# A four-group arm for expert tiles of up to 32 tokens, own index places, and a code prefetch hint

## The chip, the cores and the metric

The kernel runs on one core of a Trainium2 chip. Its time is the device time of one execution in microseconds. The engines are named as in the profile: PE (TensorE's matmuls; PEld its weight loads), DVE (VectorE), ACT (ScalarE), POOL (GpSimd) and SP (SyncE). A name with a q behind it (PEldq, SPq) is that engine's own sequencer, which works through loads of registers, branches and semaphores.

## The reference, cut to what matters

One decoder layer: a mixer (a state-space branch and an attention branch), then a mixture of experts. Only the second part is touched. 512 tokens of 1024 numbers are routed to two of sixteen experts each, with a hidden width of 512:

```python
for e in range(N_EXPERTS):
    hid = jax.nn.silu(t @ w_gate[e]) * (t @ w_up[e])
    out = out + gates[:, e:e + 1] * (hid @ w_down[e])
```

The kernel does this for the tokens that are routed to an expert alone.

## The kernel before, in words

The expert stage starts about 578 us into the span and ends near 900 us. Each expert's tokens are cut into tiles of H = 64. For each expert `body(e, 0)` always runs; `body(e, 1)` runs behind a branch on more than 64 tokens (L1354), `body(e, 2)` behind a second one, nested in it, on more than 128 (L1356). What is above 192 tokens goes through a loop that this input doesn't enter (L1421 is its branch). The counts lie in `cnti`; each engine loads the one that its branch needs into a register (L1347).

A body does this, in the order of the code:

- `tile_ranks` makes one-hot matrices on DVE (L1151) that say which token lands in which slot of a tile.
- `tile_tokens` turns them into indices and gate weights: five small matmuls on PE (L1156, L1158), a conversion (L1160) and a reduce (L1165) on DVE, and then a gather on POOL (an indirect DMA, L1161) that brings the 64 tokens of the tile, two half rows each, into `xgs`. Body 0 of expert e does it for tiles 0 and 1 of expert e + 2, body 1 for tile 2 of its own expert, whether or not that holds tokens.
- `up` multiplies the 64 tokens by gate and up (L1288). The tokens are the stationary operand, 64 columns wide; gate's product goes to the lower 64 partitions of a bank and up's to the upper 64.
- `hidden` applies silu on ACT (L1292) and multiplies on DVE (L1293). Two small copies follow (L1328, L1329), which keep the tile's indices and gate weights.
- `down` (L1303) is that of the tile before this one, and `add` scales its result (L1307) and adds it to the output by an indirect DMA on POOL (L1308).
- `x_columns` transposes gathered tokens on PE (L1181) for ACT to copy (L1182): in body 0 the first two tiles of the next expert, in body 1 tile 2 of this one. It waits for their gathers.
- `hidden_columns` transposes the hidden product (L1297) and copies it on DVE (L1298) for the next `down`.

Within a body, `in_order` keeps PE, DVE and ACT to the order of the code, save what the scheduler may place elsewhere for other engines. Between one branch and the next it can also set a body's first matmuls ahead: the first few matmuls of the next expert's `up` stand ahead of the branch L1354 on PE. The weights of the experts are loaded by SP in pieces of 1 MB, far ahead of their use, and `ew.drop` frees their places. Indices live in three sets of places used in turn (`ixs[e % 3]`), so writing one waits for the scatter that used the place before.

Of the kernel before, what the change touches and what calls it, by code (L numbers as in the profile page):

```python
# [17 lines left out]
P = 128  # L18
# [10 lines left out]
UNIT = 512  # L29
EVAC = 400  # L30
DUE = 8, 4, 4
H = P // 2
INL = 3
MAXO = 10

# [72 lines left out]
def hybrid_layer(ctx: ExitStack, tc: tile.TileContext, A, out):  # L108
# [128 lines left out]
    class Stream:  # L237
# [7 lines left out]
        def add(self, units, loads, parts):  # L245
            for n, part in enumerate(parts):
                self.parts.append((len(self.raws), n == len(parts) - 1) + part)
            self.raws.append((units, loads))
# [96 lines left out]
    class Experts:  # L345
# [18 lines left out]
        def up(self, e, k):  # L364

            assert self.nload >= 6 * e + 4
            return [self.piece(6 * e + 2 * (k // 4) + n)[:, k % 4 * FF:(k % 4 + 1) * FF] for n in range(2)]
# [750 lines left out]
    def clear_early(BM):  # L1118

        for et in kinds:  # L1120
            xgs[et] = BM.alloc(1).ap
        sgs.extend(BM.alloc(1).ap for _ in range(2))
        for a in (*xgs.values(), *sgs):
            nc.gpsimd.memset(a, 0.0)

# [14 lines left out]
        ew.raws.append(xrc[1].ap)  # L1140
        ew.load()

    ixs = [[rtile(f"ix{e}{t}", [P, 1], I32) for t in range(INL)] for e in range(3)]
    gws = [[rtile(f"gw{e}{t}", [P, 1]) for t in range(INL)] for e in range(3)]
    ixl = [rtile(f"ixl{e}", [P, 1], I32) for e in range(2)]
    gwl = [rtile(f"gwl{e}", [P, 1]) for e in range(2)]
    rkx = rtile("rkx", [P, NT])

    def onehots(oh, ranks, slots):
# [17 lines left out]
    def oh_of(e, t):  # L1167
        return ohs[t if e or t == 2 else 3 + t]
# [2 lines left out]
        onehots(oh_of(e, t), rk[:, :, e], itbs[t])  # L1171

    def tile_tokens(e, t, n0=0, n1=5):
        tokens(oh_of(e, t), lambda c: aux[:, c, e, :], ixs[e % 3][t], gws[e % 3][t], xgs[e % 2, t], n0, n1,
               128 + 8 * (e % 2 * 3 + t))

    def x_columns(xg, xT):
# [26 lines left out]

    NB = S // H - INL
    cnt = rtile("cnt", [P, 16])
    cnti = rtile("cnti", [P, 17], I32)
    ext = rtile("ext", [P, NB, 16])
    nov = rtile("nov", [P, 1])

# [6 lines left out]
    def over_counts():  # L1217
        nc.vector.tensor_copy(cnt, pc[:, 0:16])
        nc.vector.tensor_copy(cnti[:, 0:16], cnt)
        for b in range(NB):  # L1220
            nc.vector.tensor_scalar(ext[:, b, :], cnt, float((b + INL) * H) + 0.5, None, op0=ALU.is_gt)
        nc.vector.tensor_reduce(nov, ext, axis=AX.XY, op=ALU.add)
        nc.vector.tensor_copy(cnti[:, 16:17], nov)

    jk = FM.alloc(2)
    t3.append(FM.alloc(2))
# [58 lines left out]
    def up(strm, e, xT, bank):  # L1285
        for k in range(KT):
            for n, w in enumerate(strm.up(e, k)):
                nc.tensor.matmul(bank[n * H:(n + 1) * H], xT[:, (2 * (k % 4) + k // 4) * H:(2 * (k % 4) + k // 4 + 1) * H],  # L1288
                                 w, start=(k == 0), stop=(k == KT - 1))

    def hidden(bank, sg):
        nc.scalar.activation(sg[H:P], bank[0:H], AF.Silu)  # L1292
        nc.vector.tensor_tensor(sg[H:P], sg[H:P], bank[H:P], op=ALU.mult)  # L1293
# [6 lines left out]
    def down(strm, e, bank):  # L1300
        for k in range(4):
            for n, w in enumerate(strm.down(e, k)):
                nc.tensor.matmul(bank[n * H:(n + 1) * H], hidT[0][:, k, :], w, start=(k == 0), stop=(k == 3))  # L1303

    def add(bank, yo, ix, gw):

# [5 lines left out]
    def body(e, t):  # L1312

        bank, by, yo, sg = bgu[t], bys[t % 2], yos[t % 2], sgs[t % 2]
        with in_order((ET.PE, ET.DVE, ET.Activation)):
            if t == 0:
                if e + 2 < NE:
                    for u in range(2):
                        tile_ranks(e + 2, u)
                tile_ranks(e, 2)  # L1320
            if t == 1:
                tile_tokens(e, 2)
            up(ew, e, xTs[e % 2, t], bank)
            if e == 0 and t == 0:
                for e_, t_ in early:
                    tile_tokens(e_, t_, 2, 5)
            hidden(bank, sg)
            nc.vector.tensor_copy(ixl[e % 2], ixs[e % 3][t])  # L1328
            nc.vector.tensor_copy(gwl[e % 2], gws[e % 3][t])  # L1329
            if t:  # L1330
                down(ew, e, by)
                add(by, yo, ixs[e % 3][t - 1], gws[e % 3][t - 1])
            elif e:
                down(ew, e - 1, by)
                add(by, yo, ixl[1 - e % 2], gwl[1 - e % 2])
                ew.drop(2)
            if t == 0 and e + 1 < NE:
                for u in range(2):
                    x_columns(xgs[1 - e % 2, u], xTs[1 - e % 2, u])
            if t == 1:  # L1340
                x_columns(xgs[e % 2, 2], xTs[e % 2, 2])
            hidden_columns(sg)
            if t == 0 and e + 2 < NE:
                for u in range(2):
                    tile_tokens(e + 2, u)

    n_toks = [nc.values_load(cnti[0:1, e:e + 1], min_val=0, max_val=S) for e in range(NE)]  # L1347
    n_over = nc.values_load(cnti[0:1, 16:17], min_val=0, max_val=MAXO)
    n_raw = len(ew.raws)
    assert n_raw >= 18  # L1350

    for e in range(NE):
        body(e, 0)
        with tc.If(n_toks[e] > H):  # L1354
            body(e, 1)
            with tc.If(n_toks[e] > 2 * H):  # L1356
                body(e, 2)
        if e + 1 < NE:
            ew.drop(4)
    down(ew, NE - 1, bys[0])  # L1360
    add(bys[0], yos[0], ixl[(NE - 1) % 2], gwl[(NE - 1) % 2])


    spare = [ew.piece(6 * (NE - 3) + n) for n in range(18)]
# [103 lines left out]
```

## Time and profile before

| | us |
|---|---|
| median of 3 runs | 934.03 |
| lowest and highest | 932.49, 934.2 |
| the profiled execution | 932.47 |
| its span, first to last instruction | 930.6 |
| PE busy in the span | 842.8 (91%) |
| DVE busy | 540.6 (58%) |
| ACT busy | 309.6 (33%) |
| POOL busy | 101.3 (11%) |

Of the 16 DMA engines' time, queue q1 (loads that SP issues) takes 55.3% and q0 (gathers and scatters) 7.6%. The profile is one execution; a group's row gives the busy time of its instructions, the mean of one, and the idle time of the engine just ahead of them with what ended it. Matmuls are pipelined, so that records overlap: the time that a run of them takes is read from starts in the timeline, not from the sum of durations.

### The profile page before, as it was taken

The page shows a single profiled execution, that of the slowest core. Times are in us where ns is not written, and L with a number is a line of the kernel's source. Part 1 is how long each engine was busy: PE and PEld are TensorE (multiplying, and loading weights), DVE is VectorE, ACT ScalarE, POOL GpSimd, SP SyncE. Part 2 cuts the span into 40 slices and gives each one's busy share as a digit, 9 for nine tenths or more (in the row PEclk, how much of TensorE's full clock was granted, in tenths as well). Part 3 has the DMA queues.
Part 4 walks back from the last instruction along what each step waited for, and adds up shares of the span by engine and source line. Part 5 has one row for each costly group of instructions (what it writes and reads, how often), then busy time and mean ns, then how long its engine had stood idle before and what let it go on. Part 6 is the DMA issues. An engine that isn't in the chain of part 4 may idle for free. (4 is left out here: it accounts for less than half of the span.)

```text
span 930.6 us, 11855 instructions
## 1 busy us (share of the span) xinstructions
PE 842.8 (91%) x4216; PEld 542.3 (58%) x4216; DVE 540.6 (58%) x1310; ACT 309.6 (33%) x558; POOL 101.3 (11%) x113
## 2 busy tenths in 40 slices
PE   2899989999999999999999995999999999999850
PEld 1678768887666677878888883433343333333320
DVE  6849879858876687977745784423333223122216
ACT  5438788444643432432233451101110010001100
POOL 1001000000000000000000011122222221122210
PEclk9899999999999999999999985999999999999985
DMA  9951457213122248795445289598799998459734
GB/s 288 340 147 52 152 173 191 87 40 103 46 69 72 91 140 268 222 302 160 147 143 186 106 305 398 211 385 296 247 391 386 385 381 287 145 192 314 278 71 180
DMA packets 137170, 194.88 MB, mean 209 GB/s; under 512 B 11819, under 2 KB 85723, under 8 KB 137073
## 3 DMA queue, kind: packets, MB, share of 16 engines
q1 hardware_dynamic: 127040, 174.81, 55.3%
q0 software_dynamic: 9584, 18.45, 7.6%
q8 instruction: 46, 0.75, 0.3%
q10 hardware_dynamic: 464, 0.58, 0.2%
q14 instruction: 36, 0.29, 0.1%
HBM read 189.04 MB, written 13.16 MB: 217 GB/s over the span
## 5 line engine op out<-in xcount | busy, mean ns | idle before, releaser
L398 PE MATMUL bank<-rm,rm 128*128 128x512 f32 x512 | 206.2, 407 | 0.4 <-ACT rm L431 0.4
L400 PE MATMUL bank<-rm,rm 128*128 128x512 f32 x512 | 205.8, 402 | 0.0
L399 PE MATMUL bank<-rm,rm 128*128 128x512 f32 x512 | 204.8, 400 | 0.2 <-DVE rm L433 0.2
L1288 PE MATMUL bank<-fm,fm 128*64 128x512 f32 x408 | 123.8, 601 | 4.4 <-issue 2.0
L1288 PE MATMUL bank<-bm,fm 128*64 128x512 f32 x360 | 118.4, 597 | 1.6 <-PEq L1356 0.4
L234 DVE TENSOR_TENSOR rm<-fm,rm 128x1024 fp32r<-128x1024 f32 (+1 forms) x76 | 87.6, 1163 | 42.9 <-ACT rm L233 27.3
L398 PEld LDWEIGHTS bank<-rm,rm 128*128 128x128 f32 x512 | 97.8, 192 | 21.9 <-issue 3.1
L399 PEld LDWEIGHTS bank<-rm,rm 128*128 128x128 f32 x512 | 97.4, 190 | 21.5 <-issue 2.1
L400 PEld LDWEIGHTS bank<-rm,rm 128*128 128x128 f32 x512 | 97.1, 190 | 20.8 <-issue 2.3
L1293 DVE TENSOR_TENSOR bm<-bm,bank 64x512 f32<-64x512 f32 x24 | 16.6, 692 | 152.4 <-ACT bm L1292 143.4
L233 ACT CAST rm<-fm 128x1024 fp32r<-128x1024 f32 (+1 forms) x76 | 75.2, 1007 | 79.5 <-PE bank L399 59.5
L1292 ACT ACTIVATE bm<-bank 64x512 f32<-64x512 f32 x24 | 14.1, 588 | 198.8 <-PE bank L1288 198.8
L1288 PEld LDWEIGHTS bank<-fm,fm 128*64 128x64 f32 x408 | 37.9, 138 | 59.3 <-issue 58.4
L1303 PE MATMUL bank<-bm,fm 128*64 128x512 f32 x256 | 65.2, 593 | 0.7 <-DVEq L1354 0.7
L1288 PEld LDWEIGHTS bank<-bm,fm 128*64 128x64 f32 x360 | 34.7, 137 | 47.7 <-issue 46.8
L390 DVE SCALAR_TENSOR_TENSOR fm<-fm,cact,fm 128x256 f32<-128x256 f32 x112 | 51.2, 480 | 1.8
L1182 ACT COPY fm<-bank 128x512 f32<-128x512 f32 x38 | 20.9, 588 | 85.8 <-PE bank L1181 85.7
L1307 DVE SCALAR_TENSOR_TENSOR fm<-bank,fm,fm 128x512 f32<-128x512 f32 x24 | 18.0, 750 | 47.8 <-PE bank L1303 42.8
L1001 PE MATMUL bank<-rm,rm 128*128 128x512 f32 x192 | 44.2, 391 | 0.3 <-ACT fm L846 0.3
L1161 POOL DMA_INDIRECT bm<-h2d,rt_ix x38 | 39.0, 1027 | 38.9 <-DVE fm L1165 18.2
L1303 PEld LDWEIGHTS bank<-bm,fm 128*64 128x64 f32 x256 | 22.1, 137 | 35.3 <-issue 34.4
L1308 POOL DMA_INDIRECT moed<-fm,rt_ixl x16 | 25.5, 1596 | 152.2 <-DVE fm L1307 152.2
(314 smaller groups left out, 1101.7 us busy)
## 6 DMA issues: line engine op xcount, KB each, us to landing
bm<-in_w_down SPq DMA_DIRECT2D x22, 1024.0 KB
fm<-in_w_in SPq DMA_DIRECT2D x36, 512.0 KB
fm<-in_w_gate SPq DMA_DIRECT2D x17, 1024.0 KB
fm<-in_w_mod SPq DMA_DIRECT2D x16, 1024.0 KB
fm<-in_w_up SPq DMA_DIRECT2D x16, 1024.0 KB
bm<-in_w_up SPq DMA_DIRECT2D x16, 1024.0 KB
bm<-in_w_gate SPq DMA_DIRECT2D x15, 1024.0 KB
fm<-in_w_down SPq DMA_DIRECT2D x10, 1024.0 KB
```

Of the source, the lines that this page charges most:

```text
L233: ins = nc.scalar.copy(hi, src)
L234: nc.vector.tensor_tensor(lo, src, hi.bitcast(F32), op=ALU.subtract)
L390: nc.vector.scalar_tensor_tensor(acc, r, cact[:, k:k + 1], acc, op0=ALU.mult, op1=ALU.add)
L398: nc.tensor.matmul(pt, whi[:, k, :], ah.ap, start=(k == 0), stop=False)
L399: nc.tensor.matmul(pt, whi[:, k, :], al.ap, start=False, stop=False)
L400: nc.tensor.matmul(pt, wlo[:, k, :], ah.ap, start=False, stop=(k == nk - 1))
L1001: nc.tensor.matmul(wps[i][hf], sta.ap[:, tsl], mov.ap[:, hf * 512:(hf + 1) * 512], start=(k == 0 and sta is mh and mov is wh), stop=(k == ...
L1161: nc.gpsimd.indirect_dma_start(out=xg, out_offset=None, in_=h2d2, in_offset=bass.IndirectOffsetOnAxis(ap=ix[:, 0:1], axis=0), bounds_check ...
L1182: nc.scalar.copy(xT, pt)
L1288: nc.tensor.matmul(bank[n * H:(n + 1) * H], xT[:, (2 * (k % 4) + k // 4) * H:(2 * (k % 4) + k // 4 + 1) * H], w, start=(k == 0), stop=(k = ...
L1303: nc.tensor.matmul(bank[n * H:(n + 1) * H], hidT[0][:, k, :], w, start=(k == 0), stop=(k == 3))
L1308: nc.gpsimd.indirect_dma_start(out=moed2, in_=yo, in_offset=None, compute_op=ALU.add, out_offset=bass.IndirectOffsetOnAxis(ap=ix[:, 0:1], ...
```

## The change

`up` and `hidden` of each body now stand in the first arm of a branch on whether the tile holds more than Q = 32 tokens. In the second arm, `up_few` loads 32 tokens as the stationary operand and cuts each 512 columns of gate and of up into halves of 256: four products, each on 32 partitions of the bank. `hidden_few` takes silu of the two gate quarters in one instruction and multiplies in two. Since both arms are branches of their own, a body is now cut into three ordered stretches. Indices and gate weights have places of their own for each expert and tile. Sixteen registers `more` on PE say whether an expert has over 64 tokens; for experts 1 to 15 a hint behind the first matmul of body 0's `down` names that register and the branch label, so that the code of the way to be taken can be fetched.

```diff
-    ixs = [[rtile(f"ix{e}{t}", [P, 1], I32) for t in range(INL)] for e in range(3)]
+    ixa, gwa = cp.tile([P, NE, INL + 1], I32, name="ixa"), cp.tile([P, NE, INL + 1], F32, name="gwa")
+    ixs, gws = ([[a[:, e, t:t + 1] for t in range(INL)] for e in range(NE)] for a in (ixa, gwa))
+    ixl, gwl = ([a[:, e, INL:INL + 1] for e in range(NE)] for a in (ixa, gwa))
...
+        nc.vector.tensor_scalar(cnti[:, 17:33], cnt, H + 0.5, None, op0=ALU.is_gt)
...
+    def up_few(strm, e, xT, bank):
+        for k in range(KT):
+            x = xT[:, (2 * (k % 4) + k // 4) * H:(2 * (k % 4) + k // 4) * H + Q]
+            for n, w in enumerate(strm.up(e, k)):
+                for hf in range(2):
+                    o = (2 * n + hf) * Q
+                    nc.tensor.matmul(bank[o:o + Q, 0:256], x, w[:, hf * 256:(hf + 1) * 256], start=(k == 0),
+                                     stop=(k == KT - 1))
+    def hidden_few(bank, sg, tmp):
+        nc.scalar.activation(tmp[H:P, 0:256], bank[0:H, 0:256], AF.Silu)
+        for hf in range(2):
+            o = H + hf * Q
+            nc.vector.tensor_tensor(sg[H:H + Q, hf * 256:(hf + 1) * 256], tmp[o:o + Q, 0:256], bank[o:o + Q, 0:256],
+                                    op=ALU.mult)
...
             if t == 1:
                 tile_tokens(e, 2)
-            up(ew, e, xTs[e % 2, t], bank)
+        with tc.If(n_toks[e] > t * H + Q, preferred_fallthrough_block=True) as many:
+            with in_order(in_turn):
+                up(ew, e, xTs[e % 2, t], bank)
+                hidden(bank, sg)
+        with many.Else():
+            with in_order(in_turn):
+                up_few(ew, e, xTs[e % 2, t], bank)
+                hidden_few(bank, sg, sgs[2])
+        with in_order(in_turn):
...
             elif e:
-                down(ew, e - 1, by)
-                add(by, yo, ixl[1 - e % 2], gwl[1 - e % 2])
+                with tc.issue_after(down(ew, e - 1, by).ins):
+                    tc.mark_branch_hint_location(f"more{e}", more[e], engines=(ET.PE,))
+                add(by, yo, ixl[e - 1], gwl[e - 1])
...
+    more = [nc.values_load(cnti[0:1, 17 + e:18 + e], engines=(ET.PE,), min_val=0, max_val=1) for e in range(NE)]
...
-        with tc.If(n_toks[e] > H):
+        with tc.If(n_toks[e] > H, label=f"more{e}", preferred_fallthrough_block=True):
```

How the built program orders the work follows for the places where it moved. A row is one instruction (or some alike) of an engine, with its line, the tile that it writes, the tiles that it reads, the size of the result and what it waits for; `bm` and `fm` are buffers, DMASW a gather or a scatter, DMAHW a load, and after's line numbers lie some 1 to 24 higher (L1289 is `up`, L1299 `up_few`, L1321 `down`, L1345 the branch on 32 tokens, L1385 that on 64).

PE ahead of `up` of `body(1, 1)`, before: load and branch, token matmuls of tile (1, 2), then `up`.

```order
L1288 MATMUL bank_61<-bm_3762,fm_81 64x512
L1347 TENSOR_LOAD rt_cnti
L1354 COMPARE_AND_BRANCH
L1156 LDWEIGHTS fm_80
L1156 MATMUL bank_68<-fm_80 128x5 [waits DVE_49]
L1158 LDWEIGHTS fm_74
L1158 MATMUL bank_68<-fm_80,fm_74 128x5
```

PE behind the two arms of the same kind of body, now: the end of the second arm, the token matmuls, `down`, and the transposes that wait for the gather.

```order
L1299 MATMUL bank_62<-bm_3750,fm_75 32x256 x2
L1345 UNCONDITIONAL_BRANCH
L1156 LDWEIGHTS fm_80
L1156 MATMUL bank_68<-fm_80 128x5 [waits DVE_49]
L1158 LDWEIGHTS fm_74
L1158 MATMUL bank_68<-fm_80,fm_74 128x5
...
L1321 MATMUL bank_67<-bm_3751,fm_74 64x512 [waits DMAHW2_49]
L1321 MATMUL bank_67<-bm_3751,fm_74 64x512 x3
L1321 MATMUL bank_67<-bm_3752,fm_74 64x512 [waits DMAHW3_49]
L1321 MATMUL bank_67<-bm_3752,fm_74 64x512 x3
L1181 MATMUL bank_64<-ident,bm_3743 128x128 [waits DMASW7_49,Activation_49]
```

The token matmuls of tile (e, 2) have moved from ahead of `up` to behind both arms, while `x_columns` of that tile still follows `down`.

DVE in such a body, before: the conversion of the indices, then the hidden product and the two copies.

```order
L1354 COMPARE_AND_BRANCH
L1160 TENSOR_SCALAR rt_ix_3492<-bank_68,fm_80 128x1 [waits PE_49]
L1165 TENSOR_REDUCE fm_80<-bank_68 128x1
L1293 TENSOR_TENSOR bm_3752<-bm_3752,bank_62 64x512 [waits Activation_49]
L1328 COPY rt_ixl_3499<-rt_ix_3491 128x1 [waits DVE_49]
```

DVE there now: the hidden product in both arms (L1311, L1306), the copies, and then the conversion and the reduce.

```order
L1311 TENSOR_TENSOR bm_3743<-bm_3743,bank_62 64x512 [waits Activation_49]
L1345 UNCONDITIONAL_BRANCH
L1306 TENSOR_TENSOR bm_3743<-bm_3743,bank_62 32x256 [waits Activation_49]
L1306 TENSOR_TENSOR bm_3743<-bm_3743,bank_62 32x256
L1345 UNCONDITIONAL_BRANCH
L1357 COPY ixa<-ixa 128x1
L1358 COPY gwa<-gwa 128x1
L1160 TENSOR_SCALAR ixa<-bank_68,fm_80 128x1 [waits PE_49]
L1165 TENSOR_REDUCE gwa<-bank_68 128x1
```

The indices of tile (e, 2) come behind the hidden product, where they stood ahead of it; in body 0 the one-hot matrices (L1151) have moved in the same way.

PE between `x_columns` of expert 0 and its first `up`, before:

```order
L1181 MATMUL bank_65<-ident,bm_3751 128x128 [waits DMASW4_49]
L1181 MATMUL bank_65<-ident,bm_3751 128x128 x3
L1181 MATMUL bank_64<-ident,bm_3751 128x128 [waits DMASW5_49,Activation_49]
L1181 MATMUL bank_64<-ident,bm_3751 128x128 x3
L1288 MATMUL bank_61<-fm_79,fm_81 64x512 [waits DMAHW6_49,Activation_49]
```

The same place now, of sixteen loads the first one:

```order
L1181 MATMUL bank_64<-ident,bm_3742 128x128 [waits DMASW5_49,Activation_49]
L1181 MATMUL bank_64<-ident,bm_3742 128x128 x3
L1379 TENSOR_LOAD rt_cnti [waits DVE_49]
L1379 ISA x2
...
L1377 TENSOR_LOAD rt_cnti
L1345 COMPARE_AND_BRANCH
L1289 MATMUL bank_61<-fm_79,fm_81 64x512 [waits DMAHW6_49,Activation_49]
```

Sixteen loads with two register instructions each, one group of token matmuls, and the branch's own load now stand between the transposes and `up`.

## Rows read from the trace of the kernel before

**Rows 1.** The page: the span in 40 equal slices, busy tenths and PE's clock
```profile
PE   2899989999999999999999995999999999999850
...
PEclk9899999999999999999999985999999999999985
```

**Rows 2.** Windows: PE, PEld, DVE, ACT, POOL busy us; clock, DMA share, GB/s
```profile
700.00:720.00 20.00, 19.18 (x100) 8.22 (x98) 4.73 (x21) 1.66 (x3) 4.22 (x4) 1.00 1.05 385
...
820.00:840.00 20.00, 18.92 (x105) 7.67 (x103) 6.67 (x26) 2.84 (x5) 5.73 (x5) 1.00 0.39 121
```

**Rows 3.** PE's costliest groups by line and form, 578 to 900 us
```profile
L1288 PE MATMUL bank<-fm,fm 128*64 128x512 f32 x408 | 123.8, 601 | 4.4 <-issue 2.0 <-PEq L1356 1.3 <-PEq L1354 0.3
L1288 PE MATMUL bank<-bm,fm 128*64 128x512 f32 x360 | 118.4, 597 | 1.6 <-PEq L1356 0.4 <-issue 0.4 <-PEq L1354 0.3
```

**Rows 4.** PE's timeline at experts 1 and 2: start, us, engine, line, form
```profile
608.84 4.03 PE L1288 MATMUL bank<-fm,fm 128*64 128x512 f32 x17
...
616.23 1.09 PE L1181 MATMUL bank<-ident,bm 128*128 128x128 f32 x8
...
622.85 0.59 PE L1288 MATMUL bank<-bm,fm 128*64 128x512 f32 x1
622.86 0.59 PE L1288 MATMUL bank<-fm,fm 128*64 128x512 f32 x1
623.28 0.59 PE L1288 MATMUL bank<-bm,fm 128*64 128x512 f32 x1
```

**Rows 5.** PE's timeline in the mixer: short matmuls on two column groups
```profile
216.90 1.09 PE L653 MATMUL bank<-fm,fm 128*64 128x128 f32 x16
```

**Rows 6.** PE's timeline at expert 0
```profile
576.37 2.27 PE L1181 MATMUL bank<-ident,bm 128*128 128x128 f32 x8 [5.44 <-DMA bm<-h2d,rt_ix]
578.58 4.99 PE L1288 MATMUL bank<-fm,fm 128*64 128x512 f32 x17
```

**Rows 7.** Line L1347's loads: duration ns min/median/max, first and last start us
```profile
L1347 SPq TENSOR_LOAD <-rt_cnti x16: 261/262/490, 572.7 to 581.7; - x16
...
L1347 PEldq TENSOR_LOAD <-rt_cnti x16: 297/300/490, 590.8 to 891.2; - x16
```

**Rows 8.** Line L1161's landings: all gathers, then 622.2:622.4 and 792.2:792.5 alone
```profile
DMA to landing us min/median/max: 3.3/7.0/8.5
...
DMA to landing us min/median/max: 5.7/5.7/5.7
...
DMA to landing us min/median/max: 3.3/3.3/3.3
```

**Rows 9.** Timelines of ACT, DVE, POOL and PE around one tile (expert 6)
```profile
705.95 0.59 ACT L1292 ACTIVATE bm<-bank 64x512 f32<-64x512 f32 x1 [8.99 <-PE bank L1288]
...
706.57 0.69 DVE L1293 TENSOR_TENSOR bm<-bm,bank 64x512 f32<-64x512 f32 x1 [6.60 <-ACT bm L1292]
...
711.18 0.27 DVE L1160 TENSOR_SCALAR rt_ix<-bank,fm 128x1 int32<-128x1 f32 x1
711.37 0.15 DVE L1165 TENSOR_REDUCE fm<-bank 128x1 f32<-128x3 f32 x1
...
712.34 1.04 POOL L1161 DMA_INDIRECT bm<-h2d,rt_ix  x1 [0.30 <-DVE fm L1165]
...
697.44 0.17 PE L1156 MATMUL bank<-fm 128*128 128x5 bf16 x1 [0.67 <-DVE rt_ix L1160]
```

**Rows 10.** PE's branches (duration ns min/median/max), and its timeline behind expert 14's
```profile
L1354 PEldq COMPARE_BRANCH  x16: 70/316/452, 591.4 to 891.6; - x16
...
L1421 PEldq COMPARE_BRANCH  x1: 3393/3393/3393, 895.0 to 895.0; - x1
...
880.69 0.61 PE L1288 MATMUL bank<-fm,fm 128*64 128x512 f32 x1
883.17 3.22 PE L1288 MATMUL bank<-fm,fm 128*64 128x512 f32 x14 [1.86 <-issue]
```

**Rows 11.** Window 120:140 us, in the columns of rows 2
```profile
120.00:140.00 20.00, 16.58 (x102) 13.52 (x101) 15.95 (x29) 16.74 (x33) 1.43 (x3) 0.91 0.50 144
```

## Prediction before the run

> **What bounds the kernel now.** I read the page's forty slices first [rows 1]. From the 26th slice on (about 580 us) the experts run: TensorE (PE) stands at nine tenths for twelve slices, and the granted clock is full after the dip in the 24th and 25th slice. The stage's windows say the same with numbers [rows 2]: 18.9 and 19.2 us of PE in 20, DVE and ACT under 7, granted clock 1.00. So a microsecond taken off PE's path between 578 and 900 us is one off the end, as long as no other wait grows in its place. What PE does there is in the groups by line [rows 3]: 408 + 360 = 768 matmul records of gate and up (L1288, in two groups by buffer). The timeline shows how they run [rows 4]: two records start within 0.01 us of one another (gate on one half of the columns, up on the other) and the next two 0.43 us later. One tile's gate and up is 32 records, 16 pairs of 0.429 us, 6.87 us; its down has half as many, 8 pairs or 3.43 us. There are 24 tiles (768/32).
>
> The reference's routing of the drawn inputs gives the experts 31 40 95 86 27 11 40 32 91 132 170 103 25 21 59 61 tokens. In tiles of 64 that is 24 again. Ten have at most 32 tokens (experts 0, 4, 5, 7, 12, 13 whole, second tiles of 2, 3 and 8, third of 9). Ten experts skip body 1; six (2, 3, 8 to 11) run it, two of them body 2.
>
> **The change, part by part.**
>
> 1. *Four groups in ten tiles.* Each quad does 256 columns in half the time of a pair's 512, so 16 quads are 16 x 0.2147 = 3.43 us if all four run at once. Whether PE can be fed so fast: the nearest row is L653 [rows 5], 16 records of 128 columns, two groups at once, in 1.09 us with the last at 0.27: (1.09 - 0.27)/15 = 54.7 ns from start to start, with a weight load for each. 64 records at 54.7 ns are 3.50 us. I take that: 10 x (6.87 - 3.50) = **-33.7**. The other bound is no gain, 0. The Trainium skill, "TensorE: Matmul & The Clock Gate", section "Measured speedup vs the span model", speaks against a full gain: it measured three column tiles at 2.38 times one, not three. By that share (0.79) a quad would be 0.27 us and the total 8.5 us more than I forecast; the two column groups of L653 run without such a loss, and no run here shows four.
>
> 2. *Sixteen loads of `more`.* In the new order they stand on PE behind x_columns of expert 0 and ahead of the first gate and up, waiting for nothing but `cnti`. The sequencer is held in the middle of x_columns until the second gather is there, by half of 576.4 to 578.6 [rows 6] about 577.5, and goes on to the loads only then. SP loads its counts in just such a row of sixteen [rows 7]: first to last start is 9.0 us. From 577.5 that ends at 586.5, and the branch's own load and compare (0.30 and up to 0.45, [rows 7, 10], with gaps about 1.1) let up start at 587.6 instead of 578.58. PE's load alone is 0.30 us, so the lower bound is 16 x 0.30 = 4.8. Nothing is queued on PE to hide it. I take **+9.0** since the register instructions are there too.
>
> 3. *Clock at expert 0.* After its 5.44 us wait PE ran x_columns at 2.27 us against 1.09 later, and the first 17 records of up took 4.99 against 4.03 [rows 4, 6]. Nine idle microseconds more should bring the half clock back. If it lasts 4 us as now, the few arm takes 5.5 us where today's takes 6.87 + (4.99 - 4.03) = 7.8: 2.3 saved instead of 3.37, **+1.1** (0 to +2.6, if all of it runs at half, 7.0).
>
> 4. *Expert 0's jump.* Skipping bodies 1 and 2 now jumps over twice as much code (their gate and up stand there twice). Jumps of today cost 0.32 us on the sequencer as a median [rows 10], but two ran into code that wasn't there: the last one took 3.39 us, and behind expert 14's branch up stood for 1.86 us idle (883.17 - 880.69 is 2.48 where a pair takes 0.43). The hint stands for experts 1 to 15 and not for 0: **+2.4** (0 to +3.4).
>
> 5. *The other jumps.* With the hint I take them as today. Expert 14's stall goes: 0.43 - 2.48 = **-2.1** (0 to -2.1).
>
> 6. *The gather of tile (e, 2).* This is the step that decides. In body 1 the token matmuls of tile 2 stood ahead of gate and up on PE, and L1160 ahead of the hidden product on DVE. Now both stand behind the two arms, since the scheduler doesn't move work across a branch. But x_columns of that tile still follows down at once. From the end of up: silu 0.59, product 0.69, two small copies about 0.15, L1160 0.27 with the reduce 0.15, 0.30 to POOL [rows 9], that is 2.15 us, and then landing after 3.3, 7.0 (median) or 8.5 us [rows 8]; that of expert 2's tile took 5.7, of expert 10's 3.3. Meanwhile PE has the tokens (0.4) and down (3.43 + 0.1), 3.9 us. PE waits 2.15 + 5.7 - 3.9 = 3.9 us, or 1.5 with 3.3, or 5.2 with 7.0. It does so in all six experts with a body 1, filled tile or not. Before, the whole of gate and up (6.87) hid this. I take five at 3.9 and one at 1.5: **+21** (9 to 31). Queued behind x_columns on PE are the hidden transposes and all of the next tile; ACT and DVE wait with it.
>
> 7. *Branches into and out of the arms.* Body 0 ends with idle of 0.67 us at the token matmuls, which wait for L1160 [rows 9]; its load and compare lie in the middle of the next up. They now stand ahead of up, but beside that same wait for DVE, so I leave it. In the 8 tiles of bodies 1 and 2 an extra compare (0.07 to 0.45 us [rows 10]) lies before up with nothing queued: 8 x 0.4 = **+3.2** (0 to 24 x 0.45 = 10.8).
>
> 8. *Clock after the waits of 6.* In the window 120:140 [rows 11], with 3.4 us idle, the granted clock averaged 0.91, 1.8 us of 20. Two of the six waits may be as long: **+3.4** (0 to 10).
>
> 9. *Own index places.* They take waits on old scatters away from L1160; PE didn't end on them. Against this, DVE's onehots move behind the hidden product, some 2 us that end before down does. 0.
>
> Sum: -33.7 + 9.0 + 1.1 + 2.4 - 2.1 + 21 + 3.2 + 3.4 = **+4.3** on the profiled execution of 932.47 us (span 930.6 and 1.87 outside it): 936.8. That execution lies 1.56 under the median of the three runs, so the median should be about **938 us**. A measurement of this kernel can tell some 0.2% (1.9 us) from no change.
>
> **The rivals.**
>
> A, *the gathers land in time (faster).* If every late gather lands like the fastest row (3.3 us), the six waits are 9, not 21; loads at 0.30 are 4.8; no wait is long enough for the clock (-4.5) and the compares hide (-3.2): 4.3 - 12 - 4.2 - 4.5 - 3.2 = -19.6, about 914. For it: the DMA share falls to 0.39 late in the stage [rows 2], where the quick landing was seen. Against: it is 1.05 in the window at 700, and the median landing is 7.0. It decides from a landing under 1.8 us (3.9 - 2.15) for no wait at all; the whole change comes out faster once the six waits sum to under 17.
>
> B, *four groups are no faster than two.* Then 33.7 comes back: about 972. For it: no row shows four; against it: L653's rate.
>
> C, *the hint does nothing.* Then eight more jumps of 2.4 to 3.4 cost 19 to 27 and expert 14's stall stays: 959 to 967. For it: the rows show stalls of that size where code is missing, and no hint at all.
>
> D, *waits at the upper bounds.* Gathers at 7.0 (+10), every one followed by a half clock (+6.6): about 955.
>
> E, *quads a quarter slower than their columns.* 16 x 0.2147 x 1.25 is 4.3 us a tile: 0.8 more in ten, about 946. It is the case of the page in part 1; nothing in the rows is for it.
>
> **How the numbers follow.** Forecast 0.44 (930 to 946), A 0.24 (914 to 930), C 0.11, B 0.08, D 0.07, E 0.06. Range 916 to 962: it leaves out the tip of A, all of B and half of C, some 0.16. Faster by over 0.2% (under 932.2): A and the forecast's lower end, 0.24 + 0.08 = 0.32. Within 0.2%: 0.12. Slower: 0.56.
>
> **What would show it.** Right: sixteen load records on PE's sequencer behind 577 us and up starting near 587; records of 32 columns at 54 ns; PE idle in front of x_columns of tile 2, ended by a gather, in six experts, 1.5 to 5 us each. Wrong: that idle under 1 us (part 6 falls, time near 920); a tile of few that takes over 5 us (part 1); idle of over 2 us behind each outer branch (part 5); loads that end before x_columns does (part 2).

## The result, and the profile after

The changed kernel took 1004.81 us (median of 4 runs, 1001.9 to 1006.25) against 934.12 of the kernel before (4 runs beside it, 932.49 to 935.3): a ratio of 1.0754, with a 95% interval of 1.0723 to 1.0785. It is slower by 70.7 us, where 938 (916 to 962) had been forecast. The span of its profiled execution is 1000.1 us, 69.5 more than before.

The page's forty slices come first, PE's busy tenths and its granted clock, in the places of [rows 1]:

```profile
PE   2899899999999999999999535987767778786760
...
PEclk9899999999999999999999568997989998999995
```

The mixer, up to the 22nd slice, reads as before. The twelve slices of nine tenths are gone: from the 28th on PE stands at six to eight, and the clock falls under full again and again. PE's waits, from 570 to 980 us, name what it stood for (line waited at, releaser: us in total, times, longest):

```profile
PE bank L1181 <- DMA bm<-h2d,ixa: 41.1, 20, 5.1
PE bank L1156 <- DVE gwa L1165: 12.1, 14, 2.7
PE bank L1289 <- PEq L1385: 10.6, 2, 6.2
PE bank L1315 <- DVE bm L1311: 10.4, 7, 1.5
PE bank L1156 <- issue: 10.3, 1, 10.3
PE bank L1321 <- PEq L1385: 6.2, 1, 6.2
PE bank L1315 <- DVE bm L1306: 6.1, 4, 1.5
```

With the smaller rows of that list, all waits add up to 109.1 us in 70 places, where the same list of the kernel before has 18.6 in 28: 90.5 more. PE's busy time fell by only 19.1 (842.8 to 823.7), where the four groups alone should have taken 33.7 off; matmuls at a lower clock took the difference back. 90.5 - 19.1 = 71.4 is nearly the loss of 69.5.

Three of the rows had been forecast: the loads (10.3), expert 0's jump (4.4 of the 10.6), and six gathers of tile (e, 2). But L1181 is `x_columns`, and its 20 waits are two at the start (5.3 together; [rows 6] has 5.4), six of tile (e, 2) that sum to 9.2, and **twelve more, 26.6 us**, that no part of the prediction has. Nor has it the hidden transposes (L1315) that wait for DVE's product in eleven places, 16.5 us. PE's timeline at experts 4 to 6 shows where they lie (start, us, line, form, idle time ahead and what ended it):

```profile
691.79 6.44 PE L1321 MATMUL bank<-bm,fm 128*64 128x512 f32 x16 [6.24 <-PEq L1385]
698.16 1.09 PE L1181 MATMUL bank<-ident,bm 128*128 128x128 f32 x8
...
704.36 0.66 PE L1315 MATMUL bank<-ident,bm 128*128 128x128 f32 x4 [1.52 <-DVE bm L1306]
...
706.85 5.35 PE L1321 MATMUL bank<-fm,fm 128*64 128x512 f32 x16 [0.66 <-DVEq L1385]
712.96 0.63 PE L1181 MATMUL bank<-ident,bm 128*128 128x128 f32 x4 [0.76 <-DMA bm<-h2d,ixa]
714.63 0.63 PE L1181 MATMUL bank<-ident,bm 128*128 128x128 f32 x4 [1.03 <-DMA bm<-h2d,ixa]
715.29 4.06 PE L1289 MATMUL bank<-fm,fm 128*64 128x512 f32 x17
...
723.85 0.66 PE L1315 MATMUL bank<-ident,bm 128*128 128x128 f32 x4 [1.48 <-DVE bm L1311]
...
726.33 3.65 PE L1321 MATMUL bank<-bm,fm 128*64 128x512 f32 x16 [0.66 <-DVEq L1385]
732.87 0.63 PE L1181 MATMUL bank<-ident,bm 128*128 128x128 f32 x4 [2.88 <-DMA bm<-h2d,ixa]
```

Read it at 706.85: `down` of the expert before (L1321) runs first, then `x_columns` of the next expert (L1181), and only then `up` (L1289). The code has `up`, `down`, `x_columns`. The built program says the same for PE at expert 5 (the first two lines of the timeline above), behind the branch on 64 tokens of expert 4:

```
L1385 UNCONDITIONAL_BRANCH
L1321 MATMUL bank_63<-bm_3751,fm_74 64x512 x4
L1321 MATMUL bank_63<-bm_3752,fm_74 64x512 x4
L1495 BRANCH_PREFETCH_HINT
L1181 MATMUL bank_64<-ident,bm_3742 128x128 x4
L1181 MATMUL bank_65<-ident,bm_3742 128x128 x4
L1377 TENSOR_LOAD rt_cnti
L1345 COMPARE_AND_BRANCH
L1289 MATMUL bank_61<-bm_3753,fm_75 64x512
```

From expert 5 to 15 the scheduler has set `down`, the hint and `x_columns` ahead of the branch on 32 tokens (L1345) of body 0; at expert 4 it has set three of `down`'s eight matmuls there; at experts 0 to 3, nothing. The scheduler handles the new branch as one unit; nothing ties the third stretch of the body to it, so that stretch may go first (e1 adds the tie, and it no longer does). This has three effects. The gathers for `x_columns` were issued by the body before, and the `up` that hid them (6.87 us with two groups) now stands behind them. Between `up` and the hidden transposes nothing of any length is left, so PE waits for silu and product. And many of the waits are followed by matmuls at a lower clock: the `down` at 706.85 took 5.35 us at a granted clock of 0.68, where that at 726.33 took 3.65 at 1.00.

The windows around it (span, PE, PEld, DVE, ACT, POOL busy us; granted clock, DMA share, GB/s), against 1.00 in [rows 2]:

```profile
680.00:700.00 20.00, 13.10 (x80) 5.80 (x76) 5.63 (x23) 2.52 (x5) 4.34 (x4) 0.74 1.05 389
700.00:720.00 20.00, 15.19 (x116) 6.39 (x106) 4.93 (x22) 1.55 (x3) 4.55 (x4) 0.91 1.05 385
```

The branches on 64 tokens (PE's sequencer; duration ns min/median/max, first and last start):

```profile
L1385 PEldq COMPARE_BRANCH  x16: 65/342/6173, 599.2 to 962.6; - x16
```

Three of the ten jumps stalled: expert 0's (3.8 us, no hint), expert 1's (5.6) and expert 4's (6.2), which have the hint behind `up`. From expert 5 on a jump took 0.33 to 0.44.

### The profile page after: what moved, and what is told of

Same layout as the page of the kernel before. It is cut to its first block, busy times and chain, and to the rows that moved or that the text cites. A ratio compares the mean times of both kernels' runs of the same rounds, so it can differ in the third digit from the quotient of the medians.

```text
span 1000.1 us, 12776 instructions
## 1 busy us (share of the span) xinstructions
PE 823.7 (82%) x4536; PEld 537.9 (54%) x4536; DVE 540.6 (54%) x1321; ACT 308.1 (31%) x558; POOL 102.0 (10%) x114
## 3 DMA queue, kind: packets, MB, share of 16 engines
q8 instruction: 64, 1.05, 0.5%
## 4 chain that ended last, share of the span: by engine, by line
PE 51%; DMA 25%; issue 11%; DVE 8%; ACT 3%; POOL 1%; POOLq 0%; ACTq 0%; DVEq 0%; another core or an unknown queue 0%; SPq 0%
DMA moed<-fm,ixa 11%; PE bank L398 10%; PE bank L400 10%; PE bank L399 10%; DMA bm<-h2d,ixa 8%; PE bank L1289 6%; PE bank L1001 4%; DMA fm<-in_w_mod 3%; PE bank L726 2%; DVE fm L390 2%; PE bank L754 2%; DVE fm L412 1%; PE bank L744 1%; DMA fm<-rowd 1%; PE bank L653 1%
## 5 line engine op out<-in xcount | busy, mean ns | idle before, releaser
L234 DVE TENSOR_TENSOR rm<-fm,rm 128x1024 fp32r<-128x1024 f32 (+1 forms) x76 | 87.6, 1162 | 42.3 <-ACT rm L233 26.6
L1311 DVE TENSOR_TENSOR bm<-bm,bank 64x512 f32<-64x512 f32 x14 | 9.7, 692 | 137.8 <-ACT bm L1310 112.3
L1289 PE MATMUL bank<-bm,fm 128*64 128x512 f32 x208 | 72.2, 657 | 10.9 <-PEq L1385 10.6
L1289 PE MATMUL bank<-fm,fm 128*64 128x512 f32 x240 | 75.9, 626 | 1.2 <-ACTq L1387 1.1
L1321 PE MATMUL bank<-bm,fm 128*64 128x512 f32 x256 | 65.5, 650 | 11.1 <-PEq L1385 6.2
L1181 PE MATMUL bank<-ident,bm 128*128 128x128 f32 x152 | 24.2, 292 | 41.9 <-DMA bm<-h2d,ixa 41.1
L1161 POOL DMA_INDIRECT bm<-h2d,ixa x38 | 39.2, 1032 | 189.3 <-DVE gwa L1165 142.0
L1329 POOL DMA_INDIRECT moed<-fm,ixa x24 | 38.4, 1600 | 146.7 <-DVE fm L1328 142.1
L1328 DVE SCALAR_TENSOR_TENSOR fm<-bank,gwa,fm 128x512 f32<-128x512 f32 x24 | 18.0, 751 | 60.7 <-PE bank L1321 48.2
L1181 PEld LDWEIGHTS bank<-ident,bm 128*128 128x128 f32 x152 | 16.9, 146 | 60.8 <-issue 50.3
L1310 ACT ACTIVATE bm<-bank 64x512 f32<-64x512 f32 x14 | 8.3, 590 | 131.6 <-PE bank L1289 131.6
L1321 PEld LDWEIGHTS bank<-bm,fm 128*64 128x64 f32 x256 | 19.2, 148 | 46.6 <-issue 40.4
```

The costliest lines, as they stand in the source:

```text
L234: nc.vector.tensor_tensor(lo, src, hi.bitcast(F32), op=ALU.subtract)
L1161: nc.gpsimd.indirect_dma_start(out=xg, out_offset=None, in_=h2d2, in_offset=bass.IndirectOffsetOnAxis(ap=ix[:, 0:1], axis=0), bounds_check ...
L1181: nc.tensor.transpose(pt[:, b * P:(b + 1) * P], xg[:, b * P:(b + 1) * P], ident)
L1321: ins = nc.tensor.matmul(bank[n * H:(n + 1) * H], hidT[0][:, k, :], w, start=(k == 0), stop=(k == 3))
L1329: nc.gpsimd.indirect_dma_start(out=moed2, in_=yo, in_offset=None, compute_op=ALU.add, out_offset=bass.IndirectOffsetOnAxis(ap=ix[:, 0:1], ...
```

## The experiments

**e1: the move undone.** The last stretch of each body is tied to the branch block on PE, DVE and ACT: `behind` makes each of its instructions depend on that block.

```diff
-        with in_order(in_turn):
+        with in_order(in_turn), behind(nc.cur_bb.bb.instructions[-1], in_turn):
             if e == 0 and t == 0:
```

> The changed kernel with one edit: the last third of each body (down, x_columns, hidden transposes, tokens) is queued behind the branch on 32 tokens, so that the scheduler can no longer set down and x_columns ahead of it (it does from expert 5 on). Theory M (the move is the main loss): the waits of the hidden transposes for the product (16.5 us in 11 places) and those of x_columns for the next expert's gathers (some 27 us in 13 places) go, and with them the half clock behind each; only the waits for tile (e, 2) stay (9 us). The hint then stands behind up again for all experts, 6 us ahead of its jump as at experts 1 and 4, where the jump took 6.2 us: if that is the hint's doing, seven more jumps cost 6 us each and the time is about 985; if those two misses had another cause, about 945. Theory G (the gathers are too slow for short tiles in any order): x_columns still waits 2 to 3 us at most experts, over 990.

Measured: 983.79 us, ratio 1.0551 (1.0489 to 1.0614). The waits for the hidden product and for the next expert's gathers are gone; seven gather waits are left (14.6: the start's 5.4 and six of tile (e, 2), 9.2). But now all ten jumps stall. PE's waits for them:

```profile
PE bank L1300 <- PEq L1396: 32.1, 6, 6.8
PE bank L1310 <- PEq L1396: 21.4, 3, 7.3
```

Its timeline behind two of them, at experts 5 and 6:

```profile
715.86 5.46 PE L1300 MATMUL bank<-fm,fm 128*64 128x512 f32 x17 [6.78 <-PEq L1396]
...
737.55 6.13 PE L1310 MATMUL bank<-bm,fm 128*32 128x256 f32 x64 [7.28 <-PEq L1396]
```

The hint and the branch of expert 5, in the columns of the branches above:

```profile
L1506 PEldq BRANCH_PREFETCH_HINT  x1: 40/40/40, 702.9 to 702.9; - x1
...
L1396 PEldq COMPARE_BRANCH  x1: 6126/6126/6126, 708.8 to 708.8; - x1
```

So there are two causes, and in the changed kernel the first hid the second: the move that lost time also carried the hint forward, ahead of `x_columns` and `up`. In its proper place, 5.9 to 6.7 us ahead of the branch (2.5 and 2.6 at the last two experts), the hint gave nothing, as e2 shows. The 17 records behind a stall took 5.46 us where 4.03 is their full rate [rows 4], and a tile of four groups took 6.13 where one at full rate takes 3.6.

**e2: the same without hint and its sixteen loads.**

```diff
-                with tc.issue_after(down(ew, e - 1, by).ins):
-                    tc.mark_branch_hint_location(f"more{e}", more[e], engines=(ET.PE,))
+                down(ew, e - 1, by)
...
-    more = [nc.values_load(cnti[0:1, 17 + e:18 + e], engines=(ET.PE,), min_val=0, max_val=1) for e in range(NE)]
...
-        with tc.If(n_toks[e] > H, label=f"more{e}", preferred_fallthrough_block=True):
+        with tc.If(n_toks[e] > H, preferred_fallthrough_block=True):
```

> As e1_pin, and without the hint and the sixteen loads of its registers. Both theories: PE's 10.3 us behind x_columns of expert 0 go. The unhinted jump of expert 0 took 3.9 us on the sequencer in the changed kernel; ten such jumps are about 36 us where hinted ones from expert 5 on took 0.4. Theory M: 1005 - 10 - 16 - 27 - about 15 of clock - 4 (two misses of 6.2 become 3.9) + 25 = about 958. Theory G: about 985.

Measured: 987.94 us, 1.0596 (1.0466 to 1.0725); the interval includes e1's ratio. PE's waits:

```profile
PE bank L1300 <- PEq L1394: 26.9, 5, 6.8
...
PE bank L1310 <- issue: 14.2, 4, 7.3
PE bank L1310 <- PEq L1394: 13.6, 2, 6.9
PE bank L1300 <- issue: 7.4, 4, 4.0
```

The rows "issue" are counted with them: at 689.70 us PE had idled for 7.28 behind a branch of 1.28, and its sequencer shows nothing from 683.96 to the branch on 32 tokens at 689.21. That this too is a wait for code is a reading, not shown. The four rows are 62.1 us in all; e1's three rows of jumps (32.1, 21.4 and 3.0) are 56.5, and its loads are 11.2 besides. A hint behind `up` is no better than none.

**e3: the changed kernel without hint and loads, move left in.** The edit is e2's, without e1's.

> The changed kernel without the hint and its sixteen loads, nothing pinned. If the hint serves from expert 5 on: loads -10, two misses -4, seven jumps of 0.4 become 3.9, +25: about 1015. If the code would have been there without it: about 990.

Measured: 1036.9 us, 1.1121 (1.1067 to 1.1175), the slowest of all. PE stands ahead of the moved `down`, as "issue" again, and its branches on 64 tokens take up to 6.19 us:

```profile
PE bank L1321 <- issue: 42.0, 7, 10.1
```

```profile
L1383 PEldq COMPARE_BRANCH  x16: 65/902/6193, 598.1 to 994.5; - x16
```

The hint, then, did work in the changed kernel where the move had set it early: without it the jumps of the later experts stall as well.

**e4: e2, with the token matmuls ahead of the branch on 32 tokens in body 1.** This is the order of the kernel before for tile (e, 2).

```diff
+        ahead = [i.name for i in nc.cur_bb.bb.instructions if i.engine in in_turn] if t == 1 else []
         with tc.If(n_toks[e] > t * H + Q, preferred_fallthrough_block=True) as many:
...
+        for name in ahead:
+            tc.add_manual_dep(nc.cur_bb.bb.instructions[-1], name, mybir.DependencyInfo(
+                mybir.DependencyClass.NoSync, mybir.DependencyReason.DATA), reason="ahead")
```

> As e2_pin_nohint, and in body 1 the branch on 32 tokens is queued behind the token work of tile 2, so that its gather starts ahead of gate and up as in the kernel before. Theory M: the six waits for tile (e, 2), 9 us in the changed kernel, go: 9 to 12 us less than e2_pin_nohint. Theory G: 3 or less, since the gather shares its DMA queue with the others.

Measured: 981.41 us, 1.0526 (1.0457 to 1.0595). The gather waits fell from 14.6 to 5.8, of which 5.4 is the start's: 8.8 us of waits, for 6.5 us of time between two intervals that overlap. Part 6's mechanism is right, and its size is about 9.

**e5: arms in body 0 alone.** Tied as in e1, without hint and loads; bodies 1 and 2 run `up` and `hidden` as before, so that the outer jump passes over less code.

```diff
+        if t == 0:
+            with tc.If(n_toks[e] > Q, preferred_fallthrough_block=True) as many:
...
+        with in_order(in_turn), behind(arms, in_turn):
             if t == 1:
                 tile_tokens(e, 2)
...
+            if t:
                 up(ew, e, xTs[e % 2, t], bank)
                 hidden(bank, sg)
```

> The two arms in body 0 alone (six of the ten tiles of at most 32 tokens), bodies 1 and 2 as in the kernel before, the rest of a body queued behind the arms, no hint and no loads for it. What the outer branch skips is then as long as before. Theory J (the jump over doubled code is the main loss: ten stalls of 6 us and the half clock behind each): no such stall, 6 x 3.4 = 20 us gained, 16 branches at 0.5 us lost: 920 to 928. Theory G (gathers or branches eat what four groups give): 933 to 945.

Measured: 948.23 us, 1.0191 (1.0153 to 1.0229). The branches on 64 tokens fell to a median of 0.316 us (one, at expert 14, took 2.1). Instead some jumps into the second arm of body 0 stall, at experts 5, 7 and 13 (6.0 us idle at the last). PE's timeline at the first two:

```profile
678.07 0.64 PE L1310 MATMUL bank<-bm,fm 128*32 128x256 f32 x2 [6.26 <-issue]
...
712.63 5.89 PE L1310 MATMUL bank<-bm,fm 128*32 128x256 f32 x64 [6.06 <-issue]
```

**e8: jump length by itself.** The kernel before, with 128 matmuls and their weight loads, which are never executed, set inside what the branch on 64 tokens skips.

```diff
                 body(e, 2)
+                with tc.If(n_toks[e] > S - 8):
+                    up_few(ew, e, xTs[e % 2, 1], bgu[1])
+                    up_few(ew, e, xTs[e % 2, 2], bgu[2])
```

> The kernel before with dead code of some 256 matmul and weight load instructions inside the branch on over 128 tokens, behind down of body 2, under a branch that no expert takes: only the jumps get longer. Theory J: ten outer jumps at 4 to 6 us instead of 0.3, each with some clock lost behind it: 980 to 1010. If the jump's length doesn't matter: 934 to 938.

Measured: 992.31 us, 1.0647 (1.061 to 1.0684), 60 us for code that no one runs. The branches:

```profile
L1364 PEldq COMPARE_BRANCH  x16: 70/4106/6595, 591.8 to 949.2; - x16
```

PE's waits for them:

```profile
PE bank L1288 <- PEq L1364: 42.0, 9, 5.8
```

[Rows 10] have 316 ns as the median of the same branch and 452 as its longest. So the longer way over skipped code is enough, with neither arms nor move. The Trainium skill, "Runtime: NRT & Kernel Launch", section "Instruction fetch mechanics", says that a taken branch whose target lies outside the code at hand must wait for its fetch, and gives no price. These runs agree: in e8 the jump took 5.5 to 6.6 us where the DMA share during it was 0.75 or more, 4.8 at 0.58, and 3.3 to 3.4 below 0.3.

**e6: hint ahead of `up`.** e4, with hint and loads again, the hint directly behind the branch of the expert before (expert 0 has one too) and ahead of the branch on 32 tokens.

```diff
+        if t == 0:
...
+            with behind(over_of.get(e - 1), in_turn):
+                tc.mark_branch_hint_location(f"more{e}", more[e], engines=(ET.PE,))
```

> As e4_tok with hints and their sixteen loads, but the hint stands ahead of gate and up, right behind the branch of the expert before, where the changed kernel has it by chance from expert 5 on, and expert 0 has one too. Theory P (the place of the hint decides): all ten outer jumps take 0.4 us; from 981 by ten times 5.6 and about 3 of clock each less, and 10 for the loads more: about 905 to 920. If something else had made the jumps short from expert 5 on: about 985.

Measured: 947.49 us, 1.0166 (1.0126 to 1.0206). Of the ten jumps two still stall for 6.2 us and one for 2.1, the others take under 0.5, and the loads hold PE for 11.4 us at the start (a row "issue").

**e7: e6 without the row of loads.** The register for expert e + 1 is loaded inside expert e's `down`.

```diff
-    more = [nc.values_load(cnti[0:1, 17 + e:18 + e], engines=(ET.PE,), min_val=0, max_val=1) for e in range(NE)]
...
+    more = {0: more_of(0), 1: more_of(1)}
...
+                    with tc.issue_after(first.ins):
+                        more[e + 1] = more_of(e + 1)
```

> As e6_hintahead, with the register of each hint loaded one expert ahead, behind the first matmuls of down, instead of sixteen loads at the start. Theory P: 8 to 9 us less than e6_hintahead (14 of 16 loads at 0.6 us leave the path), about 900 to 912. If the load in the middle of down is not hidden there: no gain over e6_hintahead.

Measured: 938.31 us (10 runs, 933.07 to 943.22), 1.0063 (1.0038 to 1.0087): the best with the four groups, and still no faster than the kernel before. Hint and branch of expert 6, then of expert 7 (PE's sequencer):

```profile
L1525 PEldq BRANCH_PREFETCH_HINT  x1: 35/35/35, 688.3 to 688.3; - x1
...
L1414 PEldq COMPARE_BRANCH  x1: 446/446/446, 703.2 to 703.2; - x1
...
L1525 PEldq BRANCH_PREFETCH_HINT  x1: 39/39/39, 703.9 to 703.9; - x1
...
L1414 PEldq COMPARE_BRANCH  x1: 6202/6202/6202, 716.0 to 716.0; - x1
```

Here a lead of 14.9 us was enough and one of 12.1 was not. PE's waits, the longest rows:

```profile
PE bank L1167 <- DVE gwa L1176: 15.2, 23, 2.7
PE bank L1192 <- DMA bm<-h2d,ixa: 8.2, 5, 5.5
PE bank L1300 <- DMA fm<-in_w_gate: 7.0, 1, 7.0
```

Five rows of the list name weights, 16.5 us in all, and the kernel before has no such row. But the records of PE's sequencer ahead of the longest, at 723.22 us, leave no room for such a wait:

```profile
L1402 PEldq TENSOR_LOAD <-rt_cnti x1: 314/314/314, 722.6 to 722.6; - x1
...
L1365 PEldq COMPARE_BRANCH  x1: 87/87/87, 723.0 to 723.0; - x1
...
L1300 PEldq EVENT_SEMAPHORE  x1: 51/51/51, 723.1 to 723.1; - x1
```

Expert 7's jump, shown above, ends at 722.19. The load of the next count and the branch on 32 tokens follow, and the semaphore for the weights starts 0.06 us after that branch has ended. PE stood for the jump; the weights were there. The other five places of these rows read alike, with the sequencer at work up to the semaphore.

So what is new in e7 lies ahead of `up` (L1300 and L1310): 30.2 us in sixteen places, where the kernel before has 5.3 in thirteen. It is late jumps, and 0.9 to 1.5 us in eight places where no jump holds PE up for longer, since the jump, the hint, the load and the branch on 32 tokens now lie between the token matmuls and `up`; before the change the first matmuls of `up` stood ahead of the jump and covered it. In all, PE is busy 32.4 us less than before (842.8 to 810.4) and stands 35.7 longer (18.6 to 54.3): 25.0 ahead of `up`, 8.0 ahead of the token matmuls, 2.8 ahead of `x_columns`.

**e9: e7 with arms in body 0 alone.** The edit is e5's on e7.

> e7_lazy with the two arms in body 0 alone, bodies 1 and 2 as in the kernel before. In e5_body0 (the same without hints) the jump into the second arm took 5.2 us in three experts that follow a skipped one, in e7_lazy none did. If the hint ahead of up also has the code of the next body there: those three go with the half clock behind them, 948 - 16 - 9 = about 923. If it is only that the longer outer jump gave the code time: no better than e5_body0, 945 to 950.

Measured: 951.81 us, 1.019 (1.0153 to 1.0227). Hint and branch of expert 7:

```profile
L1529 PEldq BRANCH_PREFETCH_HINT  x1: 39/39/39, 712.4 to 712.4; - x1
...
L1418 PEldq COMPARE_BRANCH  x1: 6212/6212/6212, 724.5 to 724.5; - x1
```

The lead is 12.1 us, as in e7's miss. Stalls of 4.35, 6.56 and 3.66 us at experts 4, 12 and 14 have leads of 10.6, 10.7 and 11.1. But lead isn't all: expert 4's jump in e6 had 10.4 and took 0.46, with a DMA share of 0.94 over the lead, where e9's 10.6 had 0.90. Why the outer jumps need the hint here and mostly did not in e5, which skips as little, was not tried.

**e10: own index places alone,** in the kernel before.

```diff
-    ixs = [[rtile(f"ix{e}{t}", [P, 1], I32) for t in range(INL)] for e in range(3)]
-    gws = [[rtile(f"gw{e}{t}", [P, 1]) for t in range(INL)] for e in range(3)]
+    ixa, gwa = cp.tile([P, NE, INL + 1], I32, name="ixa"), cp.tile([P, NE, INL + 1], F32, name="gwa")
+    ixs, gws = ([[a[:, e, t:t + 1] for t in range(INL)] for e in range(NE)] for a in (ixa, gwa))
```

> The kernel before with own places for indices and gate weights and nothing else of the change. Both theories: within 2 us of the kernel before, since PE never waits for L1160's places there.

Measured: 934.35 us (10 runs), 1.0012 (0.9993 to 1.0031): no difference.

**e11: e7 with no tile counted as few.** The arms, branches and hints stay; every tile takes the first arm.

```diff
-        with tc.If(n_toks[e] > t * H + Q, preferred_fallthrough_block=True) as many:
+        with tc.If(n_toks[e] > t * H, preferred_fallthrough_block=True) as many:
```

> e7_lazy with the branch's limit at zero tokens of a tile, so that every tile takes gate and up on two column groups; all code, branches, loads and hints stay. It measures what four groups give where waits are mended. By PE's time alone: 33.7 us more than e7_lazy, 972. Theory W (in the run of small experts 4 to 8 the weights' loads, at full DMA share, set the pace as soon as PE is quicker; e7_lazy waits 17 us for them): those waits go, so only some 12 to 20 us more, 950 to 958.

Measured: 950.71 us, 1.0171 (1.0123 to 1.0219). Four groups in ten tiles are thus worth 12.4 us by the medians (10 by the two ratios), not 33.7. The median lies in the range of theory W, but the wait that W names isn't there: e11 too has rows of weights (6.0 us), and in all four places the sequencer is at work up to the semaphore, as in e7. What the profiles show instead is this: PE is busy 27.2 us less in e7 (810.4, against 837.6), but stands 10.3 longer ahead of `up` (30.2, against 19.9). The ten jumps take 14.6 us in e7 and 7.4 in e11, where the longer `up` of the small tiles gives six hints at experts 4 to 13 leads of 13.5 to 16.3 (11.9 to 14.9 in e7).

**e12: e6 without the tie of e1.** The hint stays ahead of `up` by its own tie, and the scheduler may move the rest again.

> e6_hintahead (947 us) without the edit that queues the last third of a body behind the branch on 32 tokens: hints, loads and token order stay as there, and the scheduler again sets down and x_columns ahead of the branch from expert 5 on. It prices that move by itself. By the changed kernel's idle time: 16.5 us of hidden transposes waiting for the product, 27 of x_columns waiting for gathers, some 10 of half clock behind them, less what would be waited for weights anyway: 975 to 1000. If the move costs nothing once all jumps are hinted: 947 to 952.

Measured: 999.84 us, 1.0689 (1.0652 to 1.0727), against e6's 1.0166: the move costs about 50 us net (52 by the medians). Its own price is rather higher, since e6 still has three late jumps (14.5 us) and e12 none. All jumps are short here, the longest 0.46 us, and the waits of the changed kernel are back:

```profile
PE bank L1192 <- DMA bm<-h2d,ixa: 40.7, 17, 5.3
...
PE bank L1326 <- DVE bm L1322: 10.4, 7, 1.5
PE bank L1326 <- DVE bm L1317: 6.1, 4, 1.5
```

## Why the prediction was wrong

The step that failed most has no term in the sum: the order of the work. Parts 6, 7 and 9 took the order that they read at experts 0 and 1 for that of all sixteen. "x_columns of that tile still follows down at once" holds, but that `down` and `x_columns` stay behind `up` does not hold in body 0 from expert 5 on. The statement "the scheduler doesn't move work across a branch" is right for work in one direction only. Work inside the cut stretches stayed on its side; the new branch itself, with both arms, was set behind work that follows it in the code. e12 against e6 prices this at some 50 us of the 70.7. The built program's order at expert 5, shown above, could have been read before any run.

Point by point:

- **1, four groups (-33.7).** The rate is right. Third tile of expert 9, timeline of the changed kernel:

```profile
808.37 2.14 PE L1299 MATMUL bank<-fm,fm 128*32 128x256 f32 x34 [0.29 <-ACT fm L1182]
810.13 0.39 PE L1299 MATMUL bank<-bm,fm 128*32 128x256 f32 x2
810.34 0.39 PE L1299 MATMUL bank<-fm,fm 128*32 128x256 f32 x2
```

  A quad starts every 0.21 us, half of the 0.43 of a pair with twice the columns, so all four groups run at once, and the tile takes 3.6 us until `down` starts at 811.96. The share lost that the Trainium skill, "TensorE: Matmul & The Clock Gate", section "Measured speedup vs the span model", has for three column tiles (2.38 times, not 3) isn't seen here with four, and rival E falls with it; so does B. (The 8.5 us that part 1 derives from that share is 8.3 by its own figures.) But the sum took it that every microsecond off PE was one off the end: with the order kept and the hints ahead of `up` it is 10 to 12 (e11 against e7). The condition that the prediction set itself, "as long as no other wait grows in its place", was not followed to the jumps: a shorter tile leaves its hint a shorter lead, and 10.3 us of what PE saves comes back ahead of `up`.
- **2, the loads (+9.0).** Right, and a little short. The sixteen run from 575.7 to 586.3, PE stands for 10.3, and `up` starts at 587.93 (forecast: 587.6). The loads' row by line, and PE's timeline behind them:

```profile
L1379 PEldq TENSOR_LOAD <-rt_cnti x16: 294/301/492, 575.7 to 586.3; - x16
```

```profile
587.02 0.18 PE L1156 MATMUL bank<-fm 128*128 128x3 bf16 x1 [10.32 <-issue]
```

- **3, the clock at expert 0 (+1.1).** The size at that tile is right: `up_few` takes 5.4 us from 587.93 on where 5.5 was forecast. But later waits lower the clock again (part 8).
- **4, expert 0's jump (+2.4).** The mechanism is right; it idled for 4.4, and the tile behind it took 2.4 us more than 6.87, at a granted clock of 0.74. PE's timeline:

```profile
603.86 9.46 PE L1289 MATMUL bank<-bm,fm 128*64 128x512 f32 x32 [4.37 <-PEq L1385]
```

- **5, the other jumps as today.** Wrong at experts 1 and 4, 6.2 us each and half clock behind, right from 5 on, by the accident of the move. This is rival C's mechanism with a wrong size: 2.4 to 3.4 was read off [rows 10], from a stretch with a DMA share of 0.31 (880 to 900 us); the two here had 0.93 and 1.06. Where the share is low, e1 has 3.6 too (0.02 at 930 us).
- **6, gathers of tile (e, 2) (+21).** Right in place and mechanism, 9.2 in size (1.2 to 2.4 each), rival A's 9. The term that was mis-sized is the landing: of the six gathers, the four whose landing the trace tells took 2.1 to 2.7 us, where 5.7 and 3.3 had been taken. (All gathers: 2.1 to 7.6, median 6.0.)
- **7, branches of the arms (+3.2).** A compare takes 0.214 us as a median, near the forecast. What was missed is the order, above, and body 0, which the part left at nothing "beside that same wait for DVE": with the order kept, e7 stands 0.9 to 1.5 us ahead of `up` in eight places even without a late jump.
- **8, clock behind waits (+3.4).** Mis-sized. PE's busy time fell by 19.1 instead of 33.7: some 14 us at a lower clock, because PE stood in 70 places (28 before), and not in six more.
- **9, own places (0).** Right (e10).

Rivals A and D changed the size of waits that were listed. No rival held that the order within a body changes from one expert to the next, which is why the measured time lies beyond all of them. The parts don't add up exactly: the move (some 50), three missed jumps (16.8 and half clock behind), the loads (10.3) and the six gathers (9.2), less 10 to 12 for the four groups, give 74 to 76 even without half clock, where 70.7 was measured; a wait that is mended uncovers another.

What stays open is what makes a hint come in time. Behind leads of 14.9 us and more every jump took under 0.9, at DMA shares up to 1.05 (e6, e7, e9). Behind leads of 11.6 to 12.1 at 1.04 and 1.05, six jumps of these runs took 1.5 to 6.2; but 10.4 sufficed once at 0.94 (e6) where 10.6 did not at 0.90 (e9). No version here beats the kernel before.

## What to carry to other kernels

Where a body is unrolled, read the built order at every instance, not at the first two; a new branch is a unit that a scheduler may set behind work that follows it, so tie that work to it. Code that is skipped has a price too: a jump that leaves the code at hand costs microseconds, and a hint helps only if it stands far enough ahead, so measure that by itself with dead code. Before counting a gain on the bounding engine, look at what its sequencer does between two runs of matmuls: a shorter run covers less of it. And where a list of waits names a DMA, check it against the sequencer's own records: in e7 the time went to a jump.

## What the runs showed of the hardware

- A taken jump over a long stretch of skipped code held PE's sequencer for 4.8 to 6.6 us at DMA shares of 0.58 to 1.06 during the jump, and for 3.3 to 3.8 below 0.3 (changed kernel, e1, e8). The share is not all: the last jump of the kernel before [rows 10] took 3.4 at 0.65. Whether the fetch shares the way with the weights was not tested by itself.
- A prefetch hint 5.9 us ahead of such a branch saved nothing (e1 beside e2); with one 14.9 us ahead the jump took 0.45 (e7).
- Four column groups of 32 columns run at the full rate: a quad of 256 columns every 0.21 us, at granted clock 1.00.
- A load of a register on PE with its two register instructions takes 0.71 us from one to the next ((586.3 - 575.7)/15), of which the load is 0.30.
- Behind waits of 1.52, 0.79 and 0.66 us the `down` at 706.85 took 5.35, at a granted clock of 0.68; behind 1.48, 0.79 and 0.66 that at 726.33 took 3.65, at 1.00. What tells the two apart was not found.
